# Moving the last group's scans behind the first dot product that follows it, and cutting the last pieces finer, in a load-bound matrix-vector kernel

## The chip, the cores and the metric

The kernel runs on one core of one Trainium2 chip. The time is the device time of one execution in microseconds (us), taken over several runs. The clock of TensorE (PE below; its passes in the tail are 0.213 or 0.108 us apart) is always called "PE's clock" in this text; the profile's "granted clock" is the share of full speed that it says PE was allowed. VectorE is DVE, ScalarE is ACT, GpSimd is POOL, SyncE is SP.

Three quantities, all read from the trace:
- the **last landing**: when the last of the 16 DMA engines signalled the semaphore of the last piece of `x` (16 signals a piece; taken from the semaphore events of the trace; no view shown here prints it);
- the **last read**: the start of DVE's last accumulator read, with which its last dot product is handed to PE;
- the **last scan**: the start of the first of the three 128-column scans that end the kernel. From there to the end of the span it is 4.16 to 4.19 us, so nothing behind it matters.

## The reference

```python
# x: 8 x 2048 x 4096, w: 4096 x 1, float32
def reference(x, w):
    proj = (x @ w).squeeze(-1)
    cm = np.maximum.accumulate(proj, axis=1)
    is_record = (proj >= cm).astype(np.float32)
    return np.cumsum(is_record, axis=1).astype(np.float32)
```

The 268 MB of `x` are read once. The arithmetic is a dot product of each row with `w`, and two running scans over 2048 values for each of 8 batches.

## The kernel before

Rows are loaded in 40 steps of 6 MB (5 groups of 8 batches, 384 rows each) into four buffers. In each step DVE takes columns 0 to 2815 of the dot products, POOL multiplies columns 2816 to 4095 and ACT adds those up. At the end of a group, PE turns the partial sums by matmuls with the identity into one row of 384 values for each batch, in PSUM (`ps`), and DVE does the scans. The last 128 rows of each batch are the tail. Batches 7 to 2 are loaded whole, 128 rows of 4096 columns each (`rows` in the code; below, each of these six is "a tail row"), then batches 1 and 0 in pieces of some columns.

```python
def scans(cm_, rec_, cnt_, n, cm0, cnt0):          # three DVE instructions
    V.tensor_tensor_scan(out=cm_, data0=ps[:B, :n], ... op0=ALU.max, op1=ALU.max)._wait_ge(psr, 1).then_inc(psr, 1)
    V.tensor_tensor(out=rec_, in0=ps[:B, :n], in1=cm_, op=ALU.is_ge)._wait_ge(psr, 2).then_inc(psr, 1)
    V.tensor_tensor_scan(out=cnt_, data0=rec_, ... op0=ALU.add, op1=ALU.add)._wait_ge(psr, 3).then_inc(cs, 1)
...
with V.Fori(0, NG):                                # DVE, the groups
    for t in range(B):
        ...                                        # three dot products of 2816 columns
    V.wait_ge(od, 16)
    scans(cm, rec, cnt, N, cm[:, N - 1 :], cnt[:, N - 1 :])
...
for m, b in enumerate(rows):                       # tail: six rows, then PIECES
    piece(slot(m)[1], (0, VC), (VC, D), st_v[:, b : b + 1], st_p[:, b : b + 1], xt[m])
for i, (b, c0, c1, v, p) in enumerate(PIECES):
    ...
a0 = next(i for i, q in enumerate(parts) if q[2] == (pa, na - 1))   # ACT's two partial sums of batch 0
a1 = next(i for i, q in enumerate(parts) if q[2] == (pa, na))
parts.insert(len(parts) - 1, parts.pop(a1))        # placed among DVE's by hand
parts.insert(len(parts) - 3, parts.pop(a0))
for k, (m, l, wait) in enumerate(parts):           # PE adds all partial sums in PSUM
    i = T.matmul(out=ps[:m, :P], lhsT=l[:, :m], rhs=identity, start=k == 0, stop=k == len(parts) - 1)
    if wait:
        i._wait_ge(*wait)
i.then_inc(psr, 1)
scans(cm_l, rec_l, cnt_l, P, cm[:, N - 1 :], cnt[:, N - 1 :])
```

Each of these float32 matmuls shows as two passes on PE in the trace (11 matmuls, x22 at L316); I count passes. The insert lines read oddly: Python takes `len(parts)` before the `pop`, so `len(parts) - 1` puts ACT's last sum at the very end, behind DVE's last one.

## Time and profile before

| | |
|---|---|
| time | 632.13 us median of 3 (631.98 to 632.36) |
| span of the profiled run, which itself took 631.60 us | 629.4 us |
| load queue | 98.8% of the 16 engines' span, 427 GB/s |
| busy share: DVE, POOL, ACT, PE | 64%, 59%, 28%, 5% |

The profiled run was faster than all three timed ones. The first lines are from the page of the kernel before: busy time by engine, then the rows of 40 slices for the granted clock of PE and for DMA, then the load queue.

```profile
PE 31.8 (5%) x98; PEld 14.4 (2%) x98; DVE 403.6 (64%) x289; ACT 177.8 (28%) x262; POOL 369.1 (59%) x137
...
PEclk9999999999999999999999999999999999999999
DMA  9999999999999999999999999999999999999995
...
q1 hardware_dynamic: 7872, 268.50, 98.8%
```

The loads fill the span from the first slice to the last but a bit. The load queue's packets take 98.8% of the 16 engines' span and move 427 GB/s. No compute engine is near its limit: DVE, the busiest, is at 64%. So a change of DVE's order can only act in the head (before the loads reach their rhythm) and in the tail, behind the last load.

The tail is in the timeline of the kernel before. Columns: start, duration, engine, line, operation, operands, count, and in brackets the engine's idle time before it with what ended it. "..." stands for lines left out.

```profile
594.44 2.73 PE L265 MATMUL ps<-identity,small 128*8 128x128 f32 x12 [113.32 <-ACT xall L123]
...
597.21 1.00 DVE L132 TENSOR_TENSOR_SCAN cm<-ps,cm,small 8x384 f32<-8x384 f32 x1 [3.60 <-PE ps L265]
...
599.76 3.05 DVE L117 CUSTOM_DVE_ANT_0 xall<-xall,w_v 128x2816 f32<-128x2816 f32 x1
...
623.98 0.54 DVE L117 CUSTOM_DVE_ANT_0 xall<-xall,w_v 128x384 f32<-128x384 f32 x1
...
624.46 0.07 DVE L117 DVE_READ_ACCUMULATOR2_ANT small<- 128x1 f32 x1
624.58 0.30 PEld L316 LDWEIGHTS ps<-identity,small 128*1 128x1 f32 x4 [0.17 <-DVE small L117]
625.22 0.47 DVE L132 TENSOR_TENSOR_SCAN cm_l<-ps,cm,small 8x128 f32<-8x128 f32 x1 [0.69 <-PE ps L316]
```

DVE stands idle for 3.60 us while PE turns the last group, then scans, and only at 599.76 starts on the tail, whose first load had landed at 589.10. From there to 624.53 it has no gap. The last landing is at 623.45 and the last read at 624.46: DVE hands over its last sum 1.01 us after the last load. The last scan follows 0.76 us later, behind four passes of PE.

One more view of the kernel before: the windows view, with each engine's busy time and in brackets its instructions, then the granted clock. Two stretches of 1 us:

```profile
core 0: us, PE busy (x) PEld busy (x) DVE busy (x) ACT busy (x) POOL busy (x), PEclk, DMA share, GB/s
623.00:624.00 1.00, 1.00 (x6) 0.29 (x4) 1.00 (x5) 0.35 (x2) 0.00 (x0) 1.00 0.01 3
624.00:625.00 1.00, 1.00 (x9) 0.51 (x8) 0.53 (x4) 0.00 (x0) 0.00 (x0) 1.00 0.06 16
```

Six matmul passes touch the first, nine the second. Single pass starts are 0.213 us apart until 624.1 and 0.108 us apart afterwards. PE's clock doubled at 624.082, in the middle of the tail, although the clock column reads 1.00 in both.

### The profile page before, as it was taken

The page shows a single profiled execution, that of the slowest core. Times are in us where ns is not written, and L with a number is a line of the kernel's source. Part 1 is how long each engine was busy: PE and PEld are TensorE (multiplying, and loading weights), DVE is VectorE, ACT ScalarE, POOL GpSimd, SP SyncE. Part 2 cuts the span into 40 slices and gives each one's busy share as a digit, 9 for nine tenths or more (in the row PEclk, how much of TensorE's full clock was granted, in tenths as well). Part 3 has the DMA queues.
Part 4 walks back from the last instruction along what each step waited for, and adds up shares of the span by engine and source line. Part 5 has one row for each costly group of instructions (what it writes and reads, how often), then busy time and mean ns, then how long its engine had stood idle before and what let it go on. Part 6 is the DMA issues. An engine that isn't in the chain of part 4 may idle for free.

```text
span 629.4 us, 1227 instructions
## 1 busy us (share of the span) xinstructions
PE 31.8 (5%) x98; PEld 14.4 (2%) x98; DVE 403.6 (64%) x289; ACT 177.8 (28%) x262; POOL 369.1 (59%) x137
## 2 busy tenths in 40 slices
PE   8000000010000001000000010000001000000102
PEld 3000000000000000000000000000000000000001
DVE  0556666677655557766666675556667766655697
ACT  1322223223322222223232322222232232322332
POOL 0556666656555555666666555556665666555865
PEclk9999999999999999999999999999999999999999
DMA  9999999999999999999999999999999999999995
GB/s 382 419 450 431 419 450 441 410 450 434 422 444 435 422 444 434 425 440 440 423 437 444 425 431 447 428 426 447 428 425 447 434 419 450 432 419 450 410 428 230
DMA packets 7891, 268.55 MB, mean 427 GB/s; under 512 B 920, under 2 KB 1352, under 8 KB 1872
## 3 DMA queue, kind: packets, MB, share of 16 engines
q1 hardware_dynamic: 7872, 268.50, 98.8%
q10 hardware_dynamic: 16, 0.02, 0.0%
q8 instruction: 1, 0.02, 0.0%
q14 instruction: 2, 0.02, 0.0%
HBM read 268.45 MB, written 0.07 MB: 427 GB/s over the span
## 4 chain that ended last, share of the span: by engine, by line
POOL 53%; issue 39%; DVE 4%; PE 3%; DMA 0%; POOLq 0%; ACT 0%; DVEq 0%; ACTq 0%; SPq 0%
POOL xall L244 53%; DVE xall L117 3%; PE w_v L203 2%; PE ps L316 1%; PE ps L265 0%; PE ps L203 0%; DMA w<-in_w_dram 0%; DVE cm L132 0%; POOLq L247 0%; ACT w L213 0%; DVE rec L136 0%; DVE cm_l L132 0%; DVE cnt_l L139 0%; DVE rec_l L136 0%; POOLq L239 0%
## 5 line engine op out<-in xcount | busy, mean ns | idle before, releaser
L117 DVE CUSTOM_DVE_ANT_0 xall<-xall,w_v 128x2816 f32<-128x2816 f32 (+3 forms) x134 | 388.8, 2951 | 186.4 <-DVEq L226 186.4
L244 POOL TENSOR_TENSOR xall<-xall,w_sb 128x1280 f32<-128x1280 f32 x120 | 345.1, 2904 | 245.9 <-POOLq L247 245.9
L123 ACT ACTIVATE xall<-xall 128x1280 f32<-128x1280 f32 x129 | 162.6, 1261 | 430.7 <-POOL xall L244 412.7
L265 PE MATMUL ps<-identity,small 128*8 128x128 f32 x60 | 13.6, 418 | 566.8 <-ACT xall L123 566.8
L286 POOL TENSOR_TENSOR xall<-xall,w_sb 128x1280 f32<-128x1280 f32 (+1 forms) x8 | 22.1, 2766 | 6.7 <-DMA xall<-in_x_dram 6.7
L123 ACT ACTIVATION_READ_ACCUMULATOR xall<-xall 128x1 f32 x129 | 24.1, 186 | 0.0
L265 PEld LDWEIGHTS ps<-identity,small 128*8 128x8 f32 x60 | 7.3, 129 | 574.1 <-ACT xall L123 570.3
L132 DVE TENSOR_TENSOR_SCAN cm<-ps,cm,small 8x384 f32<-8x384 f32 x5 | 5.0, 1004 | 17.9 <-PE ps L265 17.9
L203 PE MATMUL w_v<-w,identity 8*128 8x512 f32 x14 | 12.2, 1056 | 0.0
L117 DVE DVE_READ_ACCUMULATOR2_ANT small<- 128x1 f32 x134 | 10.8, 80 | 0.0
L221 DVE MEMSET ps<- 8x1 f32 x1 | 0.1, 59 | 16.3 <-ACT w L213 16.3
L316 PE MATMUL ps<-identity,small 128*1 128x128 f32 (+1 forms) x22 | 4.2, 363 | 23.8 <-DVE small L117 23.8
L139 DVE TENSOR_TENSOR_SCAN cnt<-rec,cnt,ps 8x384 f32<-8x384 f32 x5 | 5.0, 1001 | 0.2
L203 PEld LDWEIGHTS w_v<-w,identity 8*128 8x128 f32 x14 | 4.7, 333 | 7.3 <-issue 7.3
L210 ACT COPY w_sb<-w_v 128x768 f32<-128x768 f32 x1 | 0.8, 798 | 11.4 <-PE w_v L203 11.4
L136 DVE TENSOR_TENSOR rec<-ps,cm 8x384 f32<-8x384 f32 x5 | 2.7, 546 | 0.2
L316 PEld LDWEIGHTS ps<-identity,small 128*1 128x1 f32 (+1 forms) x22 | 1.9, 102 | 26.3 <-DVE small L117 25.5
L203 PE MATMUL ps<-w,identity 8*128 8x512 f32 x2 | 2.1, 1136 | 2.7 <-DMA w<-in_w_dram 2.7
L209 ACT ACT_TABLE_LOAD x1 | 1.3, 1283 | 1.6 <-SPq L145 1.6
L209 ACT COPY w_sb<-ps 128x512 f32<-128x512 f32 x1 | 0.6, 585 | 2.0 <-PE ps L203 2.0
L217 DVE MEMSET cm<- 8x384 f32 x1 | 0.4, 378 | 1.1 <-SPq L145 1.1
L286 POOL TENSOR_TENSOR xall<-xall,w 128x320 f32<-128x320 f32 x1 | 0.9, 867 | 0.1
(14 smaller groups left out, 4.1 us busy)
## 6 DMA issues: line engine op xcount, KB each, us to landing
xall<-in_x_dram SPq DMA_DIRECT2D x40, 6144.0 KB, 47.8
xall<-in_x_dram SPq DMA_DIRECT2D x6, 2048.0 KB, 42.8
xall<-in_x_dram SPq DMA_DIRECT2D x1, 1344.0 KB, 36.7
xall<-in_x_dram SPq DMA_DIRECT2D x2, 384.0 KB, 30.6
xall<-in_x_dram SPq DMA_DIRECT2D x1, 704.0 KB, 38.0
xall<-in_x_dram SPq DMA_DIRECT2D x1, 640.0 KB, 39.1
xall<-in_x_dram SPq DMA_DIRECT2D x2, 224.0 KB, 21.9
xall<-in_x_dram SPq DMA_DIRECT2D x1, 192.0 KB, 20.8
```

The lines of the kernel that those rows point to most:

```text
L117: return V.tensor_tensor_reduce(out=xsl, in0=xsl, in1=wsl, scale=1.0, scalar=0.0, op0=ALU.mult, op1=ALU.add, accum_out=dst,)
L123: return A.activation(out=xsl, in_=xsl, func=ACTF.Copy, accum_out=dst)
L132: V.tensor_tensor_scan(out=cm_, data0=ps[:B, :n], data1=neg.to_broadcast([B, n]), initial=cm0, op0=ALU.max, op1=ALU.max,)._wait_ge(psr, 1) ...
L136: V.tensor_tensor(out=rec_, in0=ps[:B, :n], in1=cm_, op=ALU.is_ge)._wait_ge(psr, 2).then_inc(psr, 1)
L139: V.tensor_tensor_scan(out=cnt_, data0=rec_, data1=zero.to_broadcast([B, n]), initial=cnt0, op0=ALU.add, op1=ALU.add,)._wait_ge(psr, 3).th ...
L203: i = T.matmul(out=dst, lhsT=identity[:NW, k : k + 1].to_broadcast([NW, P]), rhs=w_row, start=True, stop=True,).then_inc(bw, 1)
L209: A.copy(out=w_sb[:, CV - VC :], in_=ps)._wait_ge(bw, 1).then_inc(wc, 1)
L210: A.copy(out=w_sb[:, : CV - VC], in_=w_v[:, VC:CV])._wait_ge(bw, NW).then_inc(wc, 1)
L244: i = G.tensor_mul(out=xl, in0=xl, in1=w_sb).then_inc(pl, 1)
L265: i = T.matmul(out=ps[:B, j:N:R], lhsT=l[:, j * B : (j + 1) * B], rhs=identity, start=k == 0, stop=k == 1,)
L286: G.tensor_mul(out=xl, in0=xl, in1=w_pool(*p))._wait_ge(landed, 16).then_inc(pl, 1)
L316: i = T.matmul(out=ps[:m, :P], lhsT=l[:, :m], rhs=identity, start=k == 0, stop=k == len(parts) - 1,)
```

## The change

The intent is to have DVE start on the tail while PE is still turning the last group, and to have only a small dot product left when the last load lands. In the loop, the scans move to the head of the next group, which leaves DVE's order there as it was; the first head scans a dummy group (`ps` filled with a value below every maximum), and the last group's scans come behind the first tail row. Batch 0's last two pieces (448 and 384 columns) become three (384, 288, 160), and ACT's partial sums are placed one earlier, so that the last matmul is that of the last piece. The diff, cut to its core:

```diff
-        (0, 384, 832, (384, 832), None),
-        (0, 0, 384, (0, 384), None),
+        (0, 448, 832, (448, 832), None),
+        (0, 160, 448, (160, 448), None),
+        (0, 0, 160, (0, 160), None),
...
-        V.memset(zero, 0.0)
+        V.memset(ps[:B, :N], LOW)
+        V.memset(zero, 0.0).then_inc(psr, 1)
+
+        def group_scans():
+            V.wait_ge(od, 16)
+            scans(cm, rec, cnt, N, cm[:, N - 1 :], cnt[:, N - 1 :])
+
         with V.Fori(0, NG):
+            group_scans()
+            V.sem_inc(psr, -3)
+            V.sem_inc(od, -16)
             for t in range(B):
...
-            V.wait_ge(od, 16)
-            scans(cm, rec, cnt, N, cm[:, N - 1 :], cnt[:, N - 1 :])
-            V.sem_inc(psr, -3)
-            V.sem_inc(od, -16)
...
+            if m == 0:
+                group_scans()
...
-        parts.insert(len(parts) - 1, parts.pop(a1))
-        parts.insert(len(parts) - 3, parts.pop(a0))
+        parts.insert(len(parts) - 2, parts.pop(a1))
+        parts.insert(len(parts) - 4, parts.pop(a0))
```

The rest shifts semaphore counts by one for the dummy group, and sets only the last column of `cm` and `cnt` at the start instead of all of them.

More of the change, by code (lines that the diff above doesn't have):

```diff
@@ L16 @@
 NEG = -3.0e38
+LOW = -3.2e38
 @with_exitstack
@@ L129, in w_pool, with scans @@
         return w2[:, c0 - W2 : c1 - W2]
-    def scans(cm_, rec_, cnt_, n, cm0, cnt0):
+    def scans(cm_, rec_, cnt_, n, cm0, cnt0, base=1):
         V.tensor_tensor_scan(
@@ L134, in scans @@
             op0=ALU.max, op1=ALU.max,
-        )._wait_ge(psr, 1).then_inc(psr, 1)
+        )._wait_ge(psr, base).then_inc(psr, 1)
         V.tensor_tensor(
             out=rec_, in0=ps[:B, :n], in1=cm_, op=ALU.is_ge
-        )._wait_ge(psr, 2).then_inc(psr, 1)
+        )._wait_ge(psr, base + 1).then_inc(psr, 1)
         V.tensor_tensor_scan(
@@ L141, in scans @@
             op0=ALU.add, op1=ALU.add,
-        )._wait_ge(psr, 3).then_inc(cs, 1)
+        )._wait_ge(psr, base + 2).then_inc(cs, 1)
     NK = NG * B
@@ L163 @@
                     out=out[:, (g - 1) * N : g * N], in_=cnt
-                )._wait_ge(cs, g).then_inc(od, 16)
+                )._wait_ge(cs, g + 1).then_inc(od, 16)
         def slot(m):
@@ L186 @@
                     out=out[:, (NG - 1) * N : S0], in_=cnt
-                )._wait_ge(cs, NG).then_inc(oe, 16)
+                )._wait_ge(cs, NG + 1).then_inc(oe, 16)
         G.memset(identity, 0.0).then_inc(con, 1)
@@ L213 @@
         A.copy(out=w2, in_=w_v[:, W2 : W2 + WC]).then_inc(wc, 1)
-        A.sem_inc(od, 16)
-        V.memset(cm, NEG)
-        V.memset(cnt, 0.0)
+        A.sem_inc(od, 32)
+        V.memset(cm[:, N - 1 :], NEG)
+        V.memset(cnt[:, N - 1 :], 0.0)
         V.wait_ge(con, 3)
         V.wait_ge(wc, 3)
-        V.memset(zero, 0.0)
+        V.memset(ps[:B, :N], LOW)
[3 more added lines that the diff above has]
+            scans(cm, rec, cnt, N, cm[:, N - 1 :], cnt[:, N - 1 :])
         with V.Fori(0, NG):
+            group_scans()
+            V.sem_inc(psr, -3)
+            V.sem_inc(od, -16)
             for t in range(B):
@@ L322 @@
         i.then_inc(psr, 1)
-        scans(cm_l, rec_l, cnt_l, P, cm[:, N - 1 :], cnt[:, N - 1 :])
-        SY.dma_start(out=out[:, S0:], in_=cnt_l)._wait_ge(cs, NG + 1).then_inc(oe, 16)
+        scans(cm_l, rec_l, cnt_l, P, cm[:, N - 1 :], cnt[:, N - 1 :], 4)
+        SY.dma_start(out=out[:, S0:], in_=cnt_l)._wait_ge(cs, NG + 2).then_inc(oe, 16)
         G.wait_ge(oe, 16 * 2)
```

## The prediction

> **What bounds it now.** The load stream. The page gives one DMA queue 98.8% of the 16 engines' span and 427 GB/s for 268.45 MB read[...]. DVE is 64% busy, POOL 59%. So only the ends of the span can move: the head before the first load and the tail after the last one.
>
> **The tail before** (timeline, chain of waits, landings of the load semaphores). DVE finishes the last group at 593.6 us, waits for PE's reduction until 597.21, scans until 599.83, and only then starts the tail rows, whose first load had landed at 589.1. It then runs without a gap from 599.76 to 624.53. The last load lands at 623.45; DVE takes its piece 0.53 us later, at 623.98. After that piece: four PE passes (624.58 to 625.19), three 128-column scans to 626.50, store and shutdown to 629.4.
>
> **What the change does.**
> 1. Head: a dummy scan (1.00+0.55+1.00 us plus a 0.4 us memset) delays DVE's first dot product from 18.6 to about 21.6 us, and with it POOL. Each 14.5 us step leaves DVE 5.4 us idle, so one step absorbs it, and the load queue holds four buffers. Worth 0.
> 2. In the loop DVE's order of dots and scans stays the same. Worth 0.
> 3. Tail: the first tail row (3.0 us) fills the 3.6 us wait for PE; scans still start at about 597.2, so the last group's store and the loads queued behind it are issued as before (599.9). DVE is 3 us earlier afterwards, 602.8 instead of 605.8 after the second row, and from the sixth row on waits for loads (613.4). That is worth far less than 3 us, because the lag was only 0.5 us at the end.
> 4. Pieces: one more load, matmul and dot. Packet times (65 ns at 1536 B, 121 ns at 3072 B) give some 9 ns a packet fixed, so 8 more per engine delay the last landing by about 0.07 us (estimate), to 623.5. DVE's last pieces (0.54, 0.48, then estimates 0.37, 0.24 us start to start) run 622.45, 622.99, 623.47, 623.84, ending 624.08: 0.38 us earlier than before.
> 5. The last matmul pair is now the last piece's alone; before, a partial sum of ACT's came behind it. Two passes fewer at the end.
>
> **PE takes part of it back.** Passes were 0.213 us apart until 624.1, then 0.108. [...] the switch came 3.1 us after the tail's matmuls began (621.0). In the new order five pairs (ten passes) are ready between 623.6 and 624.2. With the switch at the same moment the last scan starts near 625.1 (0.15 earlier); if sooner, 624.8 (0.4 earlier); if PE stays slow, near 625.95, where I estimate 626.05 for before in that state. So the gain is 0.1 to 0.45 us, and which state a run gets is luck.
>
> **Prediction:** 631.8 us, 8 in 10 between 631.2 and 632.4. Faster by over 2%: 0.01; within 2%: 0.98; slower: 0.01.
>
> **What would show it.** Windows: DMA share still 1.0 until about 622.5, same end. Timeline: a tail row between the last group's dots and its scans; DVE idle before the sixth row; last piece taken within 0.4 us of its landing; one pair of PE passes after it. Head: first dot at 21.6, second step unmoved.
>
> **What would make it wrong.** Small rows (640 B) slower than estimated; a run-to-run spread (0.38 us before) as large as the gain; PE's clock state; the late first step delaying a load.

(The gain of 0.1 to 0.45 us rests on the two measured paces of PE's passes, 0.213 and 0.108 us. That the switch could come at the same moment, sooner or not at all was my assumption.)

## The result

The changed kernel took 631.86 us (median of 4, 631.32 to 632.25), the kernel before in the same rounds 632.07 (4 runs, 631.98 to 632.36). The ratio is 0.9995, with a 95% interval of 0.9978 to 1.0013: the same, within 2%.

The four runs are not spread evenly. They are 631.32, 631.47, 632.24 and 632.25: two pairs, 0.8 us apart. The median of 631.86 is the middle between the pairs, where no run lies. The profiled run is one of the slower pair, and its span is 630.1 us, longer than the 629.4 us of the kernel before. Comparing the two profiles by their spans alone would say that the change lost 0.7 us.

The timeline of the changed kernel, the lines that answer to those shown above:

```profile
593.71 3.08 DVE L120 CUSTOM_DVE_ANT_0 xall<-xall,w_v 128x2816 f32<-128x2816 f32 x1
...
594.62 2.73 PE L273 MATMUL ps<-identity,small 128*8 128x128 f32 x12 [113.27 <-ACT xall L126]
...
597.38 1.00 DVE L135 TENSOR_TENSOR_SCAN cm<-ps,cm,small 8x384 f32<-8x384 f32 x1 [0.58 <-PE ps L273]
...
613.56 3.09 DVE L120 CUSTOM_DVE_ANT_0 xall<-xall,w_v 128x2816 f32<-128x2816 f32 x1 [1.54 <-DMA xall<-in_x_dram]
...
623.92 0.32 DVE L120 CUSTOM_DVE_ANT_0 xall<-xall,w_v 128x160 f32<-128x160 f32 x1
624.16 0.08 DVE L120 DVE_READ_ACCUMULATOR2_ANT small<- 128x1 f32 x1
625.94 0.47 DVE L135 TENSOR_TENSOR_SCAN cm_l<-ps,cm,small 8x128 f32<-8x128 f32 x1 [1.70 <-PE ps L326]
```

The first tail row (593.71) fills the wait for PE, of which 0.58 us is left. DVE has caught up with the loads at the sixth row: it waits 1.54 us for DMA at 613.56. The last landing is at 623.57 and the last read at 624.16, 0.59 us later instead of 1.01. So DVE did what the change wanted. But the last scan now waits 1.70 us for PE, where it waited 0.69.

The windows view of the changed kernel says why:

```profile
623.00:624.00 1.00, 0.99 (x5) 0.30 (x5) 1.00 (x7) 0.43 (x2) 0.00 (x0) 1.00 0.12 29
624.00:625.00 1.00, 1.00 (x7) 0.59 (x5) 0.24 (x3) 0.00 (x0) 0.00 (x0) 1.00 0.00 0
625.00:626.00 1.00, 0.90 (x5) 0.30 (x3) 0.06 (x1) 0.00 (x0) 0.00 (x0) 1.00 0.00 0
```

(A count includes the passes that only reach into the stretch.) In this run PE's passes, where they follow each other without a wait, stay 0.213 us apart until the last one starts at 625.56; the clock doubled at 625.70, too late. Ten passes, of the last three pieces' sums and ACT's two, were still to do from 623.69 on. At the slow pace they start one after the other until 625.56, and the last read at 624.16 finds seven of them still waiting.

The head, in the timelines. The kernel before:

```profile
18.64 3.09 DVE L117 CUSTOM_DVE_ANT_0 xall<-xall,w_v 128x2816 f32<-128x2816 f32 x1 [0.35 <-DVEq L226]
...
33.10 3.09 DVE L117 CUSTOM_DVE_ANT_0 xall<-xall,w_v 128x2816 f32<-128x2816 f32 x1 [5.36 <-DVEq L226]
```

The changed kernel:

```profile
18.58 1.00 DVE L135 TENSOR_TENSOR_SCAN cm<-ps,cm,small 8x384 f32<-8x384 f32 x1
...
21.13 3.05 DVE L120 CUSTOM_DVE_ANT_0 xall<-xall,w_v 128x2816 f32<-128x2816 f32 x1
...
33.63 3.09 DVE L120 CUSTOM_DVE_ANT_0 xall<-xall,w_v 128x2816 f32<-128x2816 f32 x1 [3.43 <-DVEq L238]
```

The first dot product starts 2.24 us after its load landed (18.90), the second 0.27 us after its own (33.37), as in the kernel before (18.36 and 32.84, 0.28 and 0.27 us). The load itself was 0.5 us later in that run. The delay is gone after one step.

### The profile page after: what moved, and what is told of

The parts are those of the page before. It is cut to its first block, busy times and chain, and to the rows that moved or that the text cites. A ratio compares the mean times of both kernels' runs of the same rounds, so it can differ in the third digit from the quotient of the medians.

```text
span 630.1 us, 1239 instructions
## 1 busy us (share of the span) xinstructions
PE 33.4 (5%) x100; PEld 14.7 (2%) x100; DVE 406.2 (64%) x295; ACT 177.7 (28%) x262; POOL 369.2 (59%) x137
## 4 chain that ended last, share of the span: by engine, by line
POOL 52%; issue 38%; DMA 6%; PE 3%; DVE 0%; POOLq 0%; ACT 0%; SPq 0%; ACTq 0%
POOL xall L252 52%; DMA xall<-in_x_dram 6%; PE w_v L206 2%; PE ps L326 1%; PE ps L206 0%; DMA w<-in_w_dram 0%; DVE xall L120 0%; POOLq L255 0%; ACT w L216 0%; DVE cm_l L135 0%; DVE cnt_l L142 0%; SPq L176 0%; DVE rec_l L139 0%; ACT xall L126 0%; POOLq L247 0%
## 5 line engine op out<-in xcount | busy, mean ns | idle before, releaser
L326 PE MATMUL ps<-identity,small 128*1 128x128 f32 (+1 forms) x24 | 5.7, 407 | 22.9 <-DVE small L120 22.8
```

## The experiments

Theory: the scan move makes DVE end sooner after the last landing, by about 0.4 us; PE's passes behind the last sums give part or all of it back, by how much depends on where in the tail PE's clock doubles, which is luck; and the finer pieces only add passes. Rivals: the finer pieces carry the gain; the two pairs of times have nothing to do with PE's clock; the late head costs time. Twelve kernels ran, five runs each, four kernels together on one chip beside nine runs of the kernel before. All gave correct results.

| run | median, us (range) | ratio to before (95%) | last landing to last read | last read to last scan | clock doubles at |
|---|---|---|---|---|---|
| before (first runs) | 632.07 (631.98 to 632.36) | | 1.01 | 0.76 | 624.1 |
| changed (first runs) | 631.86 (631.32 to 632.25) | 0.9995 (0.9978 to 1.0013) | 0.59 | 1.78 | 625.7, too late |
| e1 scan move only | 631.77 (631.28 to 632.19) | 0.9993 (0.9980 to 1.0007) | 0.57 | 1.08 | 624.8 |
| e2 pieces only | 632.11 (631.73 to 632.64) | 0.9999 (0.9985 to 1.0012) | 1.04 | 1.56 | 625.8 |
| e3 changed, PE kept busy | 631.48 (631.21 to 632.24) | 0.9992 (0.9978 to 1.0005) | 0.58 | 0.81 | 616.8 |
| e4 before, PE kept busy | 632.24 (631.90 to 632.93) | 1.0002 (0.9988 to 1.0015) | 1.09 | 1.61 | 617.3 |
| e5 scan move, sums reordered | 631.33 (631.04 to 631.86) | 0.9989 (0.9975 to 1.0002) | 0.57 | 0.78 | 624.6 |
| e6 changed, sums reordered | 631.90 (631.43 to 632.15) | 0.9992 (0.9979 to 1.0006) | 0.58 | 1.46 | 625.4 |
| e7 e5, PE kept busy | 631.33 (631.03 to 631.88) | 0.9989 (0.9975 to 1.0002) | 0.56 | 0.56 | 613.2 |
| e8 changed, head 12 us later | 632.34 (631.54 to 632.44) | 0.9998 (0.9985 to 1.0012) | 0.58 | 1.85 | 626.5, too late |
| e9 before, PE kept busy, fewer | 631.77 (631.67 to 632.08) | 0.9993 (0.9979 to 1.0006) | 1.01 | 0.76 | 615.7 |
| e10 changed, PE kept busy, fewer | 632.48 (631.27 to 632.77) | 1.0004 (0.9991 to 1.0018) | 0.61 | 0.81 | 615.3 |
| e11 before, sums reordered | 631.78 (631.38 to 632.26) | 0.9993 (0.9980 to 1.0007) | 1.01 | 0.99 | 624.8 |
| e12 changed, again | 631.25 (631.10 to 632.51) | 0.9985 (0.9971 to 0.9998) | 0.58 | 1.86 | 626.3, too late |

The last three columns are from one profiled run each, so they show one draw of the clock; the medians average over draws. The intervals are wide against the effects, some 0.3 us of 632, so that I rest on the trace columns first, and on the runs where they fall into groups. The column "last landing to last read" does not depend on the draw, and it is the cleanest of all: 1.01 to 1.09 in every kernel with the scans in the old place, 0.56 to 0.61 in every one with the new.

### e1: the scan move alone

```diff
 against the changed kernel
-        (0, 448, 832, (448, 832), None),
-        (0, 160, 448, (160, 448), None),
-        (0, 0, 160, (0, 160), None),
+        (0, 384, 832, (384, 832), None),
+        (0, 0, 384, (0, 384), None),
...
-        parts.insert(len(parts) - 2, parts.pop(a1))
-        parts.insert(len(parts) - 4, parts.pop(a0))
+        parts.insert(len(parts) - 1, parts.pop(a1))
+        parts.insert(len(parts) - 3, parts.pop(a0))
```

> The scans moved as in the change, but the old pieces (448 and 384 columns last) and the old order of the partial sums on PE. Theory T (after the move the tail is limited by load landings and then by PE's slow passes, so the finer pieces add PE work without making DVE end sooner): DVE's last accumulator read near 624.0 to 624.2 us, as in the changed kernel (624.17); four pairs end the chain, slow passes 0.213 us apart put the last scan near 625.55 where the changed kernel has 625.94; so 631.3 to 631.9 us and at least as fast as the changed kernel. Rival R (the finer pieces carry the gain, because the last landing is followed by a smaller dot): last read later than 624.3 and slower than the changed kernel's 631.86.

Measured: 631.77 us. From the timeline of e1:

```profile
623.95 0.55 DVE L119 CUSTOM_DVE_ANT_0 xall<-xall,w_v 128x384 f32<-128x384 f32 x1
624.43 0.08 DVE L119 DVE_READ_ACCUMULATOR2_ANT small<- 128x1 f32 x1
625.51 0.47 DVE L134 TENSOR_TENSOR_SCAN cm_l<-ps,cm,small 8x128 f32<-8x128 f32 x1 [1.00 <-PE ps L325]
```

The last read was at 624.43, later than I wrote and past the mark (624.3) that I had set for the rival, because the loads were later in that run (last landing 623.86 instead of 623.57); the distance, 0.57 us, is that of the changed kernel (0.59). So the whole gain of DVE comes from the scan move, and the finer pieces add nothing to it. The reason is in the timeline: with the scans moved, DVE takes the old last piece of 384 columns (0.48 us to its read) 0.10 us after it has landed. In the changed kernel it takes the piece of 160 columns (0.24 us to its read) 0.35 us after, because the piece before, of 288 columns, still holds it. Smaller pieces end the wait for the load and begin one for DVE.

This trace is also the one to learn how to read the clock by. The windows view of e1:

```profile
623.00:624.00 1.00, 0.99 (x4) 0.10 (x4) 1.00 (x5) 0.69 (x4) 0.16 (x1) 0.50 0.03 12
624.00:625.00 1.00, 1.00 (x7) 0.56 (x7) 0.51 (x4) 0.00 (x0) 0.00 (x0) 0.58 0.08 16
```

The clock column says 0.50 here and 1.00 in the changed kernel, at the same pace of 0.213 us. In e1 the clock had already doubled at 249.4 us and fallen back some 3.4 us later, and was on record from then on. In the profiles of the kernel before and of the changed one the first record of the run is the doubling in the tail, and what lies before it is shown as full. That holds for the head too: there 14 passes of 512 columns run 0.853 us apart (four times 0.213 for four times the columns), and the column reads 1.00. The mean granted clock of e1's profiled run, 0.712, against 0.999 is that and nothing else: it says when the first record was made, not how fast PE was.

### e2: the pieces alone

```diff
 against the kernel before
-        (0, 384, 832, (384, 832), None),
-        (0, 0, 384, (0, 384), None),
+        (0, 448, 832, (448, 832), None),
+        (0, 160, 448, (160, 448), None),
+        (0, 0, 160, (0, 160), None),
...
-        parts.insert(len(parts) - 1, parts.pop(a1))
-        parts.insert(len(parts) - 3, parts.pop(a0))
+        parts.insert(len(parts) - 2, parts.pop(a1))
+        parts.insert(len(parts) - 4, parts.pop(a0))
```

> The new pieces and the new order of partial sums, the scans where they were before. Theory T: DVE arrives late as before and works without a gap (5.4 of the tail as before), last read near 624.5; the ten passes that are ready at the end then end later, last scan near 625.3 with a fast PE clock and 626.3 with a slow one; 632.1 to 632.6 us, no faster than before. Rival R: the smaller last dot ends sooner, 631.6 or less.

Measured: 632.11 us, as the kernel before in the same rounds (632.18). From the timeline of e2:

```profile
624.71 0.07 DVE L118 DVE_READ_ACCUMULATOR2_ANT small<- 128x1 f32 x1
626.26 0.47 DVE L133 TENSOR_TENSOR_SCAN cm_l<-ps,cm,small 8x128 f32<-8x128 f32 x1 [1.49 <-PE ps L317]
```

The last landing was at 623.66. From there to the last read it was 1.04 us, no shorter than 1.01, and the last scan came 1.56 us after the read. The rival (finer pieces carry the gain) is refused. From the fifth piece's landing to the last one it took 1.66 to 1.67 us in all five traces with the finer pieces and no extra matmuls, and 1.62 to 1.63 in all four with the old ones: the extra small load costs some 0.04 us.

### e3 and e4: keeping PE busy before the tail, too much of it

```diff
 e3, against the changed kernel; e4 the same against the kernel before, with (4, 20), (5, 6), (6, 6), (7, 8)
+        for n_wait, n_dummy in ((5, 20), (6, 6), (7, 8)):
+            for q in range(n_dummy):
+                i = T.matmul(
+                    out=ps[:, 384:504], lhsT=identity, rhs=identity[:, :120],
+                    start=True, stop=True,
+                )
+                if q == 0:
+                    i._wait_ge(sd, n_wait)
         for k, (m, l, wait) in enumerate(parts):
```

> The changed kernel with 34 extra matmuls of identity by identity into unused PSUM columns, issued from 611.95 us on to keep PE busy before the tail's matmuls. If PE's clock is the cause of the two groups of times (631.4 and 632.25): all runs fall in the faster group, 631.1 to 631.5, spread under 0.4 us; passes 0.108 us apart in the tail and the last scan near 625.0. If the clock is not the cause: two groups as before, or one near 631.9.

> The kernel before with 38 extra matmuls, in the same way. If the clock decides: every run like the profiled one of before (span 629.4, last scan at 625.2), 631.4 to 631.7 us, and the gain of the change at equal clock is then this less e3, 0.2 to 0.3 us. If not: 632.07 as before.

e3 measured 631.48 us and, in its profile, passes 0.109 us apart and 0.81 us from the last read to the last scan, as expected of a fast clock. The clock doubled at 616.8 us in e3 and at 617.3 in e4, where it doubled at 625.7 and 624.1 without the extra matmuls. But the runs spread over 1.03 us, not under 0.4. e4 missed: 632.24. Its trace shows my mistake: the extra passes were not done in time. The tail's own first pass started at 623.77 instead of 621.00 (in e3 at 622.20 instead of 620.19), and in e4 the queue of passes then ended last, at the fast pace. e3 and e4 therefore don't test the clock; e9 and e10 repeat them with fewer. (The edit of e4 adds 40 matmuls, not the 38 of the expectation.)

### e5 and e6: the order of the partial sums

```diff
 e5, against e1; e6 the same against the changed kernel, with (0, 1, 2, 3, 5, 6, 4, 8, 7, 9, 10, 11)
-        parts.insert(len(parts) - 1, parts.pop(a1))
-        parts.insert(len(parts) - 3, parts.pop(a0))
+        parts = [parts[q] for q in (0, 1, 2, 3, 5, 6, 4, 8, 7, 9, 10)]
```

PE takes the matmuls in the order of the program: in the changed kernel's trace no pass starts between 622.78 and 623.21, although ACT's first sum was ready at 622.88. Both kernels put ACT's sums (ready at 622.88 and 623.43 there) between or behind DVE's last ones. These two kernels put them where PE would otherwise wait.

> The scan move with the old pieces (as e1), and ACT's two partial sums matched on PE where they are ready: one after the fourth-last, one after the third-last of DVE's, so that behind DVE's last sum only its own two passes remain. Theory T (the end is DVE's last sum plus the PE passes that queue behind it): from the last accumulator read to the last scan 0.55 us with a fast PE clock and about 1.0 with a slow one, where e1 had 1.08 with a switch in the middle and the changed kernel 1.78; 631.2 to 631.6 us, 0.2 to 0.4 faster than e1. Rival (PE's queue is not what is waited for): no difference from e1, 631.8.

> The changed kernel with only the order of the partial sums changed in the same way. Theory T: from the last accumulator read to the last scan 0.6 us (fast clock) to 1.6 us (slow) instead of 0.8 and 1.78; about 631.5 to 631.7 us; not faster than e5, because it has one pair of passes more and DVE ends no sooner after the last landing (0.58 us in both). Rival (finer pieces pay once PE is out of the way): faster than e5 by 0.1 us or more.

e5 measured 631.33 us, 0.44 below e1 by the medians, though on another chip. From the last read to the last scan it is 0.78 us with the doubling 0.11 us after the last read, against 1.08 in e1 with the doubling 0.41 us after. e6 measured 631.90; with the doubling only at 625.4 its last scan came 1.46 us after the last read, where the changed kernel had 1.78 and 1.86. Both are in the range that I wrote for a slow clock to a fast one. e1 and e5 had different draws, so they don't give the worth of the order alone; e7 and e9 below do. In the same rounds e5 was not slower than e6 (means 631.42 and 631.78), so the finer pieces do not pay even with PE's order mended.

### e7: reordered, and PE kept busy with fewer extra passes

```diff
 against e5
+        for n_wait, n_dummy in ((4, 16), (5, 4), (6, 6), (7, 6)):
+            ...                                     # as in e3
...
+            for q in range({1: 2, 4: 1}.get(k, 0)):
+                T.matmul(out=ps[:1, :P], lhsT=small[:, 340:341], rhs=identity, start=False, stop=False)
```

The three matmuls of the last two lines add zero (columns of `small` that hold only zeros), to keep PE busy between the tail's own sums.

> e5 with extra matmuls on PE from 609 us on, few enough to be done before the tail's own (e3 and e4 had too many: they put the tail's first matmul off by 2.0 and 2.8 us), and three that add zero between the tail's own, to keep the clock up. Theory T: passes 0.109 us apart in the tail, last read to last scan 0.55 us in every run; 631.1 to 631.4 us, spread of the runs no more than that of the last landing, some 0.5 us. Rival: as e5.

The windows view and the timeline of e7:

```profile
623.00:624.00 1.00, 1.00 (x9) 0.33 (x8) 1.00 (x5) 0.69 (x4) 0.09 (x1) 1.00 0.05 20
624.00:625.00 1.00, 0.72 (x6) 0.13 (x4) 0.53 (x3) 0.00 (x0) 0.00 (x0) 1.00 0.00 0
```

```profile
624.30 0.08 DVE L119 DVE_READ_ACCUMULATOR2_ANT small<- 128x1 f32 x1
624.86 0.47 DVE L134 TENSOR_TENSOR_SCAN cm_l<-ps,cm,small 8x128 f32<-8x128 f32 x1 [0.47 <-PE ps L333]
```

Last read to last scan is 0.56 us, and the wait for PE 0.47, the shortest of all the profiles: two passes, 0.109 us apart, and the time from the start of the last one to the scan (0.31 us in the trace of the kernel before). e9 below has the same pieces, PE equally fast and the old order (and the scans in the old place, which acts before the last read), and takes 0.76: at equal clock the order is worth 0.20 us behind the last read, by one trace each. The span, 629.0 us, is the shortest of the profiled ones. The median is 631.33 us, the same as e5's, and the runs still spread over 0.85 us, more than I expected.

### e8: is the late head free?

```diff
 against the changed kernel
-        V.memset(ps[:B, :N], LOW)
+        for q in range(21):
+            V.memset(ps[:B, :N], LOW)._wait_ge(con, 3 + q).then_inc(con, 1)
```

> The changed kernel with 20 more memsets of 0.4 us before the first dummy scan, so that the first dot product starts near 30 us instead of 21.1. If the late head is absorbed (theory): the steps are back in the rhythm of the loads by the third or fourth, the load queue never runs dry, and the time is that of the changed kernel, 631.9 within 0.3. If the late head costs: up to 9 us more, 633 or above.

The first dot product started at 32.87 us, later than the 30 that I wrote (the memsets started 0.52 us apart, not 0.4), 14.23 us after its load, the second step 8.77 us after its own, the third 3.30, and the fourth 0.27 us, like those that follow inside a group. The last landing was at 623.71, inside the range of the other runs (623.41 to 623.92). The median, 632.34, is 0.14 above the upper edge that I wrote, 632.2; the runs are 631.54, 631.96, 632.34, 632.43 and 632.44, in the range of the changed kernel's but with more of them in its slower group, and the profiled run has the late clock (1.85 us). A cost of 12 us or of any large part of it is refused: the late head is absorbed.

### e9 and e10: the gain at equal PE clock

```diff
 e9, against the kernel before; e10 the same against the changed kernel, with (4, 16), (5, 4), (6, 6), (7, 6)
+        for n_wait, n_dummy in ((3, 16), (4, 4), (5, 6), (6, 6), (7, 6)):
+            ...                                     # as in e3
...
+            for q in range({1: 2, 4: 1}.get(k, 0)):
+                T.matmul(out=ps[:1, :P], lhsT=small[:, 340:341], rhs=identity, start=False, stop=False)
```

> The kernel before with the extra matmuls of e7's kind, so few that they are done before the tail's own (e4 failed in this). If the clock is what splits the runs of before into two groups (mean granted clock 0.998: 631.55 to 631.98; 1.0: 632.22 to 632.58): all runs near the faster group, 631.5 to 632.0; last landing to last accumulator read 1.0 us, from there to the last scan 0.76 us as in the profiled run of before.

> The changed kernel with the same fewer matmuls. Last landing to last read 0.58, last read to last scan 0.8 us (fast clock, as e3), so 0.35 to 0.45 us faster than e9 and about 0.25 us slower than e7; 631.3 to 631.6 us. This less e9 is the gain of the change at equal PE clock. If the gain in the medians came from luck with the clock alone: equal to e9.

From the timelines of e9 (the first two lines) and e10:

```profile
624.93 0.07 DVE L117 DVE_READ_ACCUMULATOR2_ANT small<- 128x1 f32 x1
625.69 0.47 DVE L132 TENSOR_TENSOR_SCAN cm_l<-ps,cm,small 8x128 f32<-8x128 f32 x1 [0.69 <-PE ps L325]
...
624.47 0.08 DVE L120 DVE_READ_ACCUMULATOR2_ANT small<- 128x1 f32 x1
625.28 0.47 DVE L135 TENSOR_TENSOR_SCAN cm_l<-ps,cm,small 8x128 f32<-8x128 f32 x1 [0.73 <-PE ps L335]
```

The last landings are at 623.92 and 623.86. e9 came out as expected: all five runs within 631.67 to 632.08, while the kernel before in the same rounds took 631.79 to 632.59, and 1.01 and 0.76 us in the profile. The profile of e10 is as expected too: 0.61 and 0.81 us, with passes 0.109 us apart. At equal, fast clock the change is thus worth (1.01 + 0.76) - (0.61 + 0.81) = 0.35 us from the last landing to the last scan. But only the profiled run of e10 was fast (631.27); the other four took 632.06 to 632.77, slower than the changed kernel itself. There are no traces of those, so what made them slow stays open. So for the changed kernel neither e3 nor e10 shows that keeping PE busy removes the slower group of times; for the kernel before, e9 does.

### e11: the order of the sums alone

```diff
 against the kernel before
-        parts.insert(len(parts) - 1, parts.pop(a1))
-        parts.insert(len(parts) - 3, parts.pop(a0))
+        parts = [parts[q] for q in (0, 1, 2, 3, 5, 6, 4, 8, 7, 9, 10)]
```

> The kernel before with only the partial sums reordered as in e5. Theory: DVE's part unchanged (1.0 us from the last landing to the last read), PE's part 0.55 (fast) to 1.1 us (slow); 631.5 to 632.0 us, so half of e5's gain over before comes from the order alone and the rest from the scan move.

Measured: 631.78 us against 632.27 in the same rounds, with DVE's part unchanged (1.01) and PE's at 0.99, the doubling 0.36 us after the last read. So the order of two matmuls gives about as much, by the medians, as the scan move alone (e1: 631.77 against 632.18). The interval of each ratio still holds 1, and e11's trace does not show the gain: its way from the last landing to the last scan, 2.00 us, is longer than the 1.77 of the kernel before, whose clock had doubled earlier. The 0.20 us at equal clock (e7 against e9) is the firmer number.

### e12: the changed kernel again

> The changed kernel unaltered, for more runs of it on one chip beside e10: two groups again, near 631.4 with a mean granted clock of 0.998 and near 632.2 with 1.0, median between them by luck, 631.6 to 632.2.

The five runs are 631.10, 631.22, 631.25, 631.42 and 632.51. Four fall in the faster group, so the median is 631.25, below the 631.6 to 632.2 that I wrote, and the ratio 0.9985 (0.9971 to 0.9998). The profiled run is the slow one, with the doubling at 626.3.

### The two groups, counted

The changed kernel ran nine times in all: six runs within 631.10 to 631.47 and three within 632.24 to 632.51, none between. Its two traces are both of the slower group, and both have the slow pace to the end. The kernel before ran 27 times beside the experiments. By the mean granted clock that each run lists: 0.998 in four runs, 631.55 to 631.98; 1.0 in ten runs, 632.22 to 632.59. I read a mean of 0.998 there as a clock that doubled early enough to fall back well before the end (the profile of the kernel before, 0.999, has it up at 624.08 and back at 0.50 from 627.50 on, with the end at 629.4), and a mean of 1.0 as one that doubled very late (626.3 in e12's profile, which reads 1.0) or never. (With other kernels the label is not clean, and never where it is 0.6 to 0.8: see e1. A run of e12 with 1.0 took 631.25; and the profiles of e9 and e10, where the clock doubled at 615.7 and 615.3 and the tail's passes were fast, read 1.0 too.) If the clock is what parts them, its draw is worth about 0.6 us in the kernel before (means 632.44 and 631.80; the 13 runs with other labels, left out, lie from 631.77 to 632.97) and 1.0 us in the changed one (means 632.33 and 631.30, parted by their times). No run of the changed kernel's faster group was traced, but the traces give the same size: from the last landing to the last scan 2.37 and 2.44 us with the late clock (the changed kernel, e12), 1.39 and 1.42 with the fast one (e3, e10). Later loads don't explain it: the last landings of the two slow traces, 623.57 and 623.75, are the earlier ones (623.84 and 623.86 in e3 and e10).

Over all runs the means are 632.17 us for the kernel before (31 runs) and 631.64 for the changed one (9 runs), 0.53 us apart; within the same rounds the difference is 0.30 in the first ones and 0.67 beside e12.

## Why the prediction was right

It gave 631.8 us, 631.2 to 632.4, and 98% for "within 2%"; measured were 631.86 us. "The same, within 2%" was nearly sure: 2% is 12.6 us, and all that follows the last landing takes 5.9 us in the profile before. That the median came within 0.06 us of 631.8 is luck: no run lies there, and e12, the same kernel, had a median of 631.25. What can be judged is the mechanism, point by point:

1. **The head is worth 0.** Right. The first dot product started at 21.1 us (written: about 21.6), and one step absorbed it. e8 put it off to 32.9 us, and three steps absorbed that.
2. **The loop is unchanged.** Right: from the second step on, dot products start 0.27 us after their loads land in both traces, except at a group's head, 1.01 to 1.04 us.
3. **The first tail row fills the wait for PE, and DVE then waits for loads from the sixth row on.** Right, to 0.2 us: scans at 597.38, the wait at 613.56. And the sentence that 3 us won there are worth far less at the end holds: the distance from the last landing to the last read fell by 0.42 us, from 1.01 to 0.59.
4. **The finer pieces end DVE 0.38 us earlier.** The size is right (0.30 us by the trace, 0.42 from the last landing, which came 0.12 later); the place in the sum is not. The prediction books it under the pieces, and they have no part in it: e1 has the whole of it (0.57) with the old pieces, and e2 none of it (1.04) with the new ones. The extra load cost 0.04 us where I estimated 0.07.
5. **Two passes fewer at the end.** They are fewer behind the last sum, but the passes queue: at the slow pace the queue of ten from 623.69 on decides, whatever the order inside it. e6 (1.46 us behind the last read against 1.78 and 1.86, all at a late clock) and e7 against e9 show that the order counts when ACT's sums are taken out of that queue and put where PE waits.
6. **PE takes part back, and which state a run gets is luck.** Right, and the larger effect of all. The estimate for a slow clock was a last scan near 625.95; measured 625.94 and, in e12, 626.19 with a landing 0.18 us later. In different runs of nearly the same tail the doubling falls anywhere between 624.1 and 626.5. Once up, the clock stayed up for 3.413 us both in the kernel before (624.082 to 627.496) and in the changed one (625.700 to 629.114). With matmuls put before the tail it came earlier (613.2 to 617.3 in e3, e4, e7, e9 and e10); what else sets the moment is not shown.

The gain was put at 0.15 us with the doubling at the same moment as before and at 0.4 with an earlier one; e9 and e10, fast throughout, measure 0.35 in one trace each. At a slow clock it was put at 0.1 us (626.05 against 625.95); the ten and three slow runs differ by 0.11 us in the mean, though the ten were picked by label and the three by time. The overall 0.53 us is more than either, perhaps because six of nine runs of the changed kernel drew the fast clock, judged by their times, against fewer of the kernel before. Whether the change makes that draw likelier (its tail matmuls start 0.8 us earlier, at 620.19 instead of 621.00) or nine runs are too few, the runs do not settle.

**A version that beats both?** e5 and e7 have the lowest means of the variants, 631.42 and 631.40 us, 0.7 us below the kernel before in the same rounds, and none of their ten runs is above 631.88, while the changed kernel's slower group is at 632.2 to 632.5. But against the changed kernel's mean of nine runs, 631.64, on other chips, that is no proof, and each interval against the kernel before just holds 1. What is shown is the mechanism: e7's trace has the shortest way from the last load to the last scan, 1.12 us against 1.77 before and 2.37 in the changed kernel's profiled run.

## What to carry to other kernels

In a load-bound kernel, measure the tail from the last landing, engine by engine, before and after a change: spans of single runs mix it with later loads and with PE's clock, and here they would have shown a loss for what at equal clock is a gain of 0.35 us. Cut the last pieces finer only while the consumer is idle when they land; beyond that, each piece adds work to the engines behind (here DVE took the old last piece 0.10 us after it landed, and the finer ones left the way to the last read at 0.59 us against 0.57). And when sums from several engines meet in one accumulation, put each where it is ready, so that behind the last one nothing queues (0.56 us from the last read to the last scan in e7, 0.76 in e9).
